# A row softmax on one core: waits put inside the instructions of VectorE and GpSimd, and two 16-row transfers joined into one of 32 rows, in each direction

## The chip, the core and the metric

The kernel runs on one core of a Trainium2 chip. The metric is the device time of one execution in microseconds (us). The kernel before took 159.75 us, the median of three runs (159.71, 159.75 and 159.80). One more execution was profiled, and it took 160.0 us. All engines start together and meet only through semaphores: VectorE (DVE), ScalarE (ACT), GpSimd (POOL) and SyncE (SP), which here only issues transfers. 16 DMA engines move the data.

## What is computed

The input x has 16 x 1024 rows of 512 float32 values. Each row gets its softmax:

```
x_max = np.max(x, axis=-1, keepdims=True)
exp_x = np.exp(x - x_max)
return (exp_x / np.sum(exp_x, axis=-1, keepdims=True)).astype(np.float32)
```

That is 33.55 MB read and 33.55 MB written, and each value is touched once on the way.

## The kernel before, in words

**Tiling.** The 16,384 rows stand as 128 rows in each of 128 partitions. "Row" below means such a row index, 0 to 127, and stands for 128 rows of x. Computation goes by groups of 8 rows: 16 groups, g = 0 to 15, each 128 x 4096 values. Transfers go by blocks of 16 rows (`BLOCKS`): 8 loads and 8 stores of 4096 KB. Within a block one partition's rows lie side by side in DRAM (`in_dram`), so a block of 16 rows is 128 contiguous runs of 32 KB, one run for each partition. One buffer, `held`, keeps 96 rows per partition, 192 KB (`RING = 96`), and everything is done in place in it. Rows 96 to 127 take the places of rows 0 to 31, once those are stored.

**The four steps of a group.** VectorE takes the negative row maximum (`reduce_max`, L168). ScalarE computes exp(x - max) row by row, eight ACTIVATE instructions per group, and adds up the row sums as it goes (the loop at L194 to L199). VectorE takes the reciprocal of the sums (L174). Then GpSimd (groups 0 to 11) or VectorE (groups 12 to 15) multiplies the group by its reciprocals (`tensor_mul`, L176).

**The order of the work** is written out by hand. `ORDER` is the sequence in which SP issues the transfers. The first `AHEAD` entries are loads that wait for nothing; one of them is put ahead of the starting barrier. `AFTER` holds two stores back until a later group is scaled. `VECTOR` is VectorE's sequence, where Mg is the maximum of group g, Pg its reciprocal when GpSimd scales the group, and Vg its reciprocal and the scaling by VectorE itself:

```
AHEAD = 6
AFTER = {(0, 16): 4, (48, 64): 11}
VECTOR = """
    M0 M1 P0 M2 P1 M3 P2 M4 P3 M5 P4 M6 P5 M7 P6 M8 P7 M9 P8 M10 P9 M11
    P10 P11 M12 M13 V12 M14 V13 M15 V14 V15
"""
```

So the store of rows 0 to 15 is issued once group 4 is scaled too, and the store of rows 48 to 63 once group 11 is. SP issues strictly in this order: a store that waits for its groups holds back whatever stands behind it. The load of rows 96 to 111 waits until rows 0 to 15 are stored, and the load of rows 112 to 127 until rows 16 to 31 are.

**Waits.** `take(engine, semaphore, n)` (L114) is an instruction of its own: the engine waits until the semaphore holds at least n, and takes n off it. VectorE has 28 of these: 8 for loads (`loaded`), 16 ahead of the reciprocals (`expd`, which ScalarE raises once per group) and 4 ahead of its own `tensor_mul` (`to_vector`). GpSimd has 12 (`to_pool`), one ahead of each `tensor_mul`. VectorE's own busy instructions are 36: 16 maxima, 16 reciprocals and 4 multiplications.

Of the kernel before, what the change touches and what calls it, by code (L numbers as in the profile page):

```python
# [1 line left out]

# [4 lines left out]

F32 = mybir.dt.float32
EXP = mybir.ActivationFunctionType.Exp
AX = mybir.AxisListType.X  # L10

GROUP = 8
GROUPS = 16
RING = 12 * GROUP

BLOCKS = [(0, 16), (16, 32), (32, 48), (48, 64), (64, 80), (80, 96), (96, 112), (112, 128)]
ORDER = [
    ("L", (0, 16)),
    ("L", (16, 32)),
    ("L", (32, 48)),
    ("L", (48, 64)),
    ("L", (64, 80)),
    ("L", (80, 96)),
    ("S", (0, 16)),
    ("S", (16, 32)),  # L30
    ("S", (32, 48)),
    ("L", (96, 112)),
    ("L", (112, 128)),
    ("S", (48, 64)),
    ("S", (64, 80)),
    ("S", (80, 96)),
    ("S", (96, 112)),
    ("S", (112, 128)),
]
AHEAD = 6  # L40

# [9 lines that stand above are left out]
AT_HEAD = {mybir.EngineType.SP: 1}  # L53

def loads_at_the_head(nc):

    main, body = nc.main_func.blocks[0], nc.main_func.blocks[1]
    for engine, count in AT_HEAD.items():  # L60
        loads = [
            i
            for i in body.instructions
            if i.engine == engine and type(i).__name__ == "InstDMACopy"
        ][:count]
        barrier = next(
            n
            for n, i in enumerate(main.instructions)
            if i.engine == engine and type(i).__name__ == "InstDrain"
        )  # L70
        for load in loads:
            body.instructions.remove(load)
        main.instructions[barrier:barrier] = loads


@with_exitstack
def kernel(
    ctx: ExitStack,
    tc: tile.TileContext,
    x: bass.AP,  # L80
    out: bass.AP,
):
    nc = tc.nc
    nc.at_finalize(loads_at_the_head)
    P = nc.NUM_PARTITIONS

    d = x.shape[-1]
    x_rows, out_rows = x.flatten_outer_dims(), out.flatten_outer_dims()
    assert x_rows.shape[0] == GROUPS * GROUP * P

    def in_dram(rows, a, b):

        first, last = next(k for k in BLOCKS if k[0] <= a and b <= k[1])
        block = rows[first * P : last * P].rearrange("(p r) d -> p r d", p=P)
        return block[:, a - first : b - first, :]

    held = nc.alloc_sbuf_tensor("held", [P, RING, d], F32).ap()
    shift = nc.alloc_sbuf_tensor("shift", [P, GROUPS * GROUP], F32).ap()
    sums = nc.alloc_sbuf_tensor("sums", [P, GROUPS * GROUP], F32).ap()
    recip = nc.alloc_sbuf_tensor("recip", [P, GROUPS * GROUP], F32).ap()  # L100

    loads = [k for what, k in ORDER if what == "L"]
    stores = [k for what, k in ORDER if what == "S"]
    loaded = {k: nc.alloc_semaphore(f"loaded{k[0]}") for k in loads}
    scaled = [nc.alloc_semaphore(f"scaled{g}") for g in range(GROUPS)]
    stored = {k: nc.alloc_semaphore(f"stored{k[0]}") for k in stores}
    maxed = nc.alloc_semaphore("maxed")
    expd = nc.alloc_semaphore("expd")
    to_pool = nc.alloc_semaphore("to_pool")
    to_vector = nc.alloc_semaphore("to_vector")  # L110

    def take(engine, semaphore, n):

        engine.wait_ge(semaphore, n).then_inc(semaphore, -n)  # L114

    def rows(a, b):
        assert a // RING == (b - 1) // RING
        return held[:, a % RING : (b - 1) % RING + 1, :]

    def meets(k, a, b):  # L120
        return k[0] < b and a < k[1]

    def group(g):
        return g * GROUP, (g + 1) * GROUP

    def stats(t, g):
        return t[:, g * GROUP : (g + 1) * GROUP]

    def load(k):
        copy = nc.sync.dma_start(out=rows(*k), in_=in_dram(x_rows, *k))  # L130
        copy.then_inc(loaded[k], 16)
        return copy

    with tc.manual_schedule():
        for _, k in ORDER[:AHEAD]:
            tc.no_tile_sem_insts.add(load(k).ins.name)
    tc.close()  # L140
    tc.compile()  # L141

    taken, done = set(), set()
    for what, k in ORDER[AHEAD:]:
        if what == "L":
            for s in stores:
                if meets(s, k[0] - RING, k[1] - RING) and s not in taken:
                    take(nc.sync, stored[s], 16)
                    taken.add(s)
            load(k)  # L150
        else:
            for g in range(GROUPS):
                if (meets(k, *group(g)) or AFTER.get(k) == g) and g not in done:
                    take(nc.sync, scaled[g], 1)
                    done.add(g)
            nc.sync.dma_start(out=in_dram(out_rows, *k), in_=rows(*k)).then_inc(
                stored[k], 16
            )


    seen = set()

    def rowmax(g):
        for k in loads:
            if meets(k, *group(g)) and k not in seen:
                take(nc.vector, loaded[k], 16)
                seen.add(k)
        nc.vector.reduce_max(  # L168
            out=stats(shift, g), in_=rows(*group(g)), axis=AX, negate=True
        ).then_inc(maxed, 1)  # L170

    def scale(g, engine, ready):
        take(nc.vector, expd, 1)
        nc.vector.reciprocal(out=stats(recip, g), in_=stats(sums, g)).then_inc(ready, 1)  # L174
        take(engine, ready, 1)
        engine.tensor_mul(  # L176
            out=rows(*group(g)),
            in0=rows(*group(g)),
            in1=stats(recip, g).unsqueeze(2).to_broadcast([P, GROUP, d]),
        ).then_inc(scaled[g], 1)  # L180

    for step in VECTOR.split():
        what, g = step[0], int(step[1:])
        if what == "M":
            rowmax(g)
        elif what == "V":
            scale(g, nc.vector, to_vector)
        else:
            scale(g, nc.gpsimd, to_pool)


    nc.scalar.preload_act_table(EXP)  # L192

    with nc.scalar.Fori(0, GROUPS) as i:  # L194
        take(nc.scalar, maxed, 1)
        for r in range(GROUP):
            row = held[:, bass.ds(i % (RING // GROUP) * GROUP + r, 1), :]
            at = bass.ds(i * GROUP + r, 1)
            act = nc.scalar.activation(  # L199
                out=row,  # L200
                in_=row,
                func=EXP,
                bias=shift[:, at],
                scale=1.0,
                accum_out=sums[:, at],
            )
        act.then_inc(expd, 1)


    for k in stores:  # L210
        if k not in taken:
            take(nc.sync, stored[k], 16)


# [1 line left out]
_INS = ['x']  # L216
_OUTS = [((16, 1024, 512), 'float32')]


# [23 lines left out]
```

## Time and profile before

| What | Value |
|---|---|
| profiled execution, its own time | 160.0 us |
| its span, from the first instruction to the last | 158.7 us |
| median of three runs | 159.75 us |
| VectorE busy | 90.1 us (57%), 36 instructions |
| ScalarE busy | 92.0 us (58%), 257 instructions |
| GpSimd busy | 83.9 us (53%), 16 instructions |
| DMA | 2305 packets, 67.12 MB, mean 423 GB/s |

The span ends with SP's wait for the last store; 1.3 us of the profiled execution's time lie outside it. An engine's busy time leaves out its waits and the instructions that only issue transfers. The DMA lines count packets over all 16 engines: each 4096 KB transfer shows as 128 packets of 32768 bytes, 8 on each DMA engine, and 16 packets of 4 bytes, one on each DMA engine, that raise the semaphore of the transfer. The trace records start, duration and size of every packet, and the time at which each transfer has landed (its 16th raise of the semaphore).

For finding one's way by time: the loads land at 12.41, 22.10, 31.81, 41.52, 51.24 and 60.95 us (rows 0 to 95), 99.98 (rows 96 to 111) and 109.69 (rows 112 to 127). The stores land at 70.65, 80.31 and 90.27 us (rows 0 to 47), then at 119.38, 129.22, 139.33, 149.00 and 158.65 us (rows 48 to 127).

### The profile page before, as it was taken

What the parts mean: (1) busy time and instruction counts of PE and PEld (TensorE: products, weight loads), DVE (VectorE), ACT (ScalarE), POOL (GpSimd) and SP (SyncE); (2) the same over time, 40 slices, a digit from 0 to 9 for tenths busy, and PEclk for the clock granted to TensorE, in tenths of its full rate; (3) what the DMA queues carried; (4) which work ended last, traced back from release to release, by engine and by line L of the source; (5) the groups of instructions that cost most, each with busy time, mean ns of one, the idle gap of its engine ahead of it and who ended that gap; (6) DMA issues with size and microseconds to landing.
All of it is one profiled execution on the core that took longest, in us unless ns stands there. A gap on an engine that the chain in (4) does not pass through costs nothing. (4 is left out here: it accounts for less than half of the span.)

```text
span 158.7 us, 747 instructions
## 1 busy us (share of the span) xinstructions
DVE 90.1 (57%) x36; ACT 92.0 (58%) x257; POOL 83.9 (53%) x16
## 2 busy tenths in 40 slices
DVE  0008959778877977977700000794999996820000
ACT  0300699999999999999994000059936749000000
POOL 0000009999999999999999999990000000000000
DMA  8999999999999999999999999999999999999996
GB/s 264 446 463 413 405 463 446 405 430 479 413 396 454 454 413 396 479 446 396 430 479 413 396 396 396 479 446 396 405 520 396 396 446 473 396 405 512 405 405 264
DMA packets 2305, 67.12 MB, mean 423 GB/s; under 512 B 256, under 2 KB 256, under 8 KB 256
## 3 DMA queue, kind: packets, MB, share of 16 engines
q1 hardware_dynamic: 2304, 67.11, 98.9%
q14 instruction: 1, 0.01, 0.0%
HBM read 33.55 MB, written 33.55 MB: 423 GB/s over the span
## 5 line engine op out<-in xcount | busy, mean ns | idle before, releaser
L199 ACT ACTIVATE held<-held,shift x128 | 90.3, 709 | 39.1 <-ACTq L114 39.1
L176 POOL TENSOR_TENSOR held<-held,recip 128x4096 f32<-128x4096 f32 x12 | 83.7, 7018 | 23.2 <-POOLq L114 23.2
L168 DVE TENSOR_REDUCE shift<-held 128x8 f32<-128x4096 f32 x16 | 70.3, 4401 | 27.2 <-DVEq L114 27.2
L199 ACT ACTIVATION_READ_ACCUMULATOR held<-held,shift x128 | 24.2, 189 | 0.0
L176 DVE TENSOR_TENSOR held<-held,recip 128x4096 f32<-128x4096 f32 x4 | 17.7, 4424 | 0.6
L174 DVE RECIPROCAL recip<-sums 128x8 f32<-128x8 f32 x16 | 3.2, 202 | 22.0 <-DVEq L114 22.0
L192 ACT ACT_TABLE_LOAD x1 | 1.3, 1283 | 3.9 <-PEq L141 3.9
L227 POOL MEMSET const-float32-0.0<- 128x1 f32 x1 | 0.1, 99 | 0.2 <-issue 0.2
L227 POOL MEMSET const-bfloat16-1.0<- 128x1 bf16 x1 | 0.1, 103 | 0.0
L227 POOL MEMSET const-uint8-127<- 128x1 uint8 x1 | 0.1, 102 | 0.0
L227 POOL MEMSET const-float32-1.0<- 128x1 f32 x1 | 0.1, 99 | 0.0
## 6 DMA issues: line engine op xcount, KB each, us to landing
held<-in_x_dram SPq DMA_DIRECT2D x8, 4096.0 KB, 30.0
out_dram<-held SPq DMA_DIRECT2D x8, 4096.0 KB, 21.1
```

What stands on the lines that cost most here:

```text
L168: nc.vector.reduce_max(out=stats(shift, g), in_=rows(*group(g)), axis=AX, negate=True).then_inc(maxed, 1)
L174: nc.vector.reciprocal(out=stats(recip, g), in_=stats(sums, g)).then_inc(ready, 1)
L176: engine.tensor_mul(out=rows(*group(g)), in0=rows(*group(g)), in1=stats(recip, g).unsqueeze(2).to_broadcast([P, GROUP, d]),).then_inc(scal ...
L192: nc.scalar.preload_act_table(EXP)
L199: act = nc.scalar.activation(out=row, in_=row, func=EXP, bias=shift[:, at], scale=1.0, accum_out=sums[:, at],)
L227: nc = _bacc.Bacc("TRN2", target_bir_lowering=False, num_devices=1)
```

## The change

Two things are edited. First, the transfers: rows 64 to 95 are one block instead of two, so one load of 8192 KB stands where two of 4096 KB stood, and one store likewise; one run in DRAM for this block is 64 KB long. `AHEAD` is 5, since the same six blocks' worth of rows is now five loads.

Second, the waits: a reciprocal waits for `expd` itself (`wait_op` on the instruction), and a `tensor_mul` waits itself for `to_pool` or `to_vector`. The semaphores are no longer lowered after each wait but count up, so the g-th wait asks for a higher value, and one `take` for each of the three semaphores at the end lowers them to zero. The waits for loads remain instructions of their own, 7 now. VectorE's waits of their own fall from 28 to 9, GpSimd's from 12 to 1.

```diff
-BLOCKS = [(0, 16), (16, 32), (32, 48), (48, 64), (64, 80), (80, 96), (96, 112), (112, 128)]
+BLOCKS = [(0, 16), (16, 32), (32, 48), (48, 64), (64, 96), (96, 112), (112, 128)]
...
-    ("L", (64, 80)),
-    ("L", (80, 96)),
+    ("L", (64, 96)),
...
-    ("S", (64, 80)),
-    ("S", (80, 96)),
+    ("S", (64, 96)),
...
-AHEAD = 6
+AHEAD = 5
...
-    seen = set()
+    seen, given = set(), {}
...
     def scale(g, engine, ready):
-        take(nc.vector, expd, 1)
-        nc.vector.reciprocal(out=stats(recip, g), in_=stats(sums, g)).then_inc(ready, 1)
-        take(engine, ready, 1)
+        nc.vector.reciprocal(out=stats(recip, g), in_=stats(sums, g)).wait_op(
+            expd, g + 1, "sem-ge"
+        ).then_inc(ready, 1)
+        given[ready] = given.get(ready, 0) + 1
         engine.tensor_mul(
             out=rows(*group(g)),
             in0=rows(*group(g)),
             in1=stats(recip, g).unsqueeze(2).to_broadcast([P, GROUP, d]),
-        ).then_inc(scaled[g], 1)
+        ).wait_op(ready, given[ready], "sem-ge").then_inc(scaled[g], 1)
...
+    take(nc.vector, expd, GROUPS)
+    take(nc.vector, to_vector, given[to_vector])
+    take(nc.gpsimd, to_pool, given[to_pool])
```

Order and number of the busy instructions are the same on every engine; SP issues 14 transfers instead of 16.

## Prediction, made before the changed kernel ran

> **What bounds the kernel now.** I first read the page's span and its DMA queues:
>
> ```profile
> span 158.7 us, 747 instructions
> q1 hardware_dynamic: 2304, 67.11, 98.9%
> q14 instruction: 1, 0.01, 0.0%
> ```
>
> The data queue keeps 16 DMA engines busy for 98.9% of the span, while no compute engine passes 58%. The second line is the bound; the third, a single packet of instructions, matters below. Next the busy time by stretch, to see whether the DMA engines ever run dry:
>
> ```profile
> core 0: us, DVE busy (x) ACT busy (x) POOL busy (x), PEclk, DMA share, GB/s
> ...
> 20.00:60.00 40.00, 31.37 (x15) 40.00 (x115) 36.33 (x6) 1.00 1.00 433
> 60.00:85.00 25.00, 15.38 (x8) 25.00 (x72) 25.00 (x4) 1.00 1.01 434
> 85.00:95.00 10.00, 0.20 (x1) 0.13 (x2) 10.00 (x3) 1.00 1.03 419
> ...
> 140.00:157.00 17.00, 0.00 (x0) 0.00 (x0) 0.00 (x0) 1.00 1.00 432
> ```
>
> The last columns: a DMA share of 1.00 and 432 to 434 GB/s, with VectorE busy or not. Only 85 to 95 us is slower (419): packets there last up to 2.17 us, on all 16 engines at once. So a compute engine counts only where it issues a transfer too late. There are two tight places. The store of rows 0 to 15 is issued at 58.69 (group 4 scaled); the first DMA engine to finish the loads goes on with it at 59.80 and the last at 60.51. The store of rows 48 to 63 is issued at 107.50 (group 11); its first packets start at 108.99. From issue to first packet the first load took 1.02 us, so the slack is 0.09 to 0.80 us in the first place and 0.47 us or more in the second.
>
> The chain of waits ends on VectorE at 139.9 and says nothing here: the last store is issued at 140.0 and queues behind others until 158.65.
>
> **How the DMA engines end.** In the packet records an engine starts a 32 KB packet every 1.21 us (1.213 long, overlapping the next by 4 ns), a semaphore packet of 9 ns costs its engine 5 ns, and 14 engines end between 157.40 and 157.68 us. Two are late: one ends at 157.91, one at 158.23, and the kernel ends with that one (landing at 158.65). Its history shows why. At 130.94 it took the instruction packet:
>
> ```profile
> q1 hardware_dynamic: 15, 0.49, 94.8%
> q14 instruction: 1, 0.01, 1.6%
> ```
>
> (DMA view, 130.0 to 131.2 us.) This 8192-byte packet took 0.309 us, the next data packet began 0.306 us late and took 1.564 us instead of 1.213: 0.66 us in all. Stepping back from its end at 158.23 by 1.21 us a packet leads exactly to that packet. Without it this engine would have ended at 157.57, and the last would be the one at 157.91, which collects small delays (14 to 69 ns a packet) during stores.
>
> **Who fetches instructions at 130.94?** By the instruction records GpSimd had run its last instruction by then (started 100.39), SP had waited since 125, and ScalarE was in the 16th turn of a loop whose first 15 turns fetched nothing. VectorE had started its 66th of 70 at 129.14:
>
> ```profile
> 128.80 0.19 DVE L174 RECIPROCAL recip<-sums 128x8 f32<-128x8 f32 x1
> 129.14 4.42 DVE L176 TENSOR_TENSOR held<-held,recip 128x4096 f32<-128x4096 f32 x1
> 135.13 0.20 DVE L174 RECIPROCAL recip<-sums 128x8 f32<-128x8 f32 x1 [1.56 <-DVEq L114]
> ```
>
> It also has the longest program without a loop. So I take the fetch as VectorE's, set off by the count of instructions that it has passed. That is inferred, not shown.
>
> **The change part by part.**
>
> *Waits inside instructions.* VectorE loses 16 + 4 waits and one load's wait, and gains two at the end: 70 records become 51. It never comes to a 66th, so no fetch falls in the span (SP goes from 47 to 44, GpSimd from 40 to 29). The end moves from 158.23 to 157.91: **-0.32 us**. Bounds: 0, if the fetch is another engine's; -0.66, if the engine at 157.91 catches up too.
>
> A wait instruction of its own costs about 0.11 us ahead of a reciprocal (23.11 to 23.22). GpSimd's come early, under the instruction before: its multiplications start 6.975 us apart and last
>
> ```profile
> L176 POOL TENSOR_TENSOR held<-held,recip x12: 7017/7018/7019, 23.7 to 100.4; 128x4096 f32<-128x4096 f32 x12
> ```
>
> so they already run without a gap. At most the chain starts 0.1 to 0.2 us earlier, and the two tight stores with it. They queue behind loads anyway: 0. Behind a waiting GpSimd instruction stand only its later multiplications; behind VectorE's waiting reciprocal stand the maxima that stood behind the wait before.
>
> *The load.* The same bytes in the same queue land together at about 60.95, so rows 64 to 79 come 9.7 us later. Group 8's maximum, at 57.22 before, starts at 61.1 and ends at 65.5; group 7's reciprocal behind it moves from 62.71 to 65.5. GpSimd needs it at 72.50: 7.0 us spare. ScalarE starts group 8 about 3 us late and stays so through group 11, whose reciprocal moves from 85.27 to about 88.5; GpSimd wants it at 100.39. Group 12 waits for its load (99.98) in any case. Cost 0; it would show only if the load came over 6 us later still.
>
> *The store.* Rows 64 to 95 are scaled by 107.4, and both old stores were issued by 108.5, behind the store of rows 48 to 63. Cost 0. The freed SP time (0.34 us per issue, 1.00 for the third) hid under transfers: 0.
>
> *Packets.* If a 64 KB run is one packet, each DMA engine has 16 fewer data packets and 2 fewer semaphore packets. The trace has no 64 KB packet. The nearest row for a packet's fixed cost is the semaphore packet: 9 ns long, 5 ns of its engine's time. 18 x 5 ns = **-0.09 us**; ends of the range for this part 0 and -0.16 (18 x 9 ns). The other way, long packets might run slower: the slowest stretch (419 against 433 GB/s, 3.2%) over 32 of 128 packets, 38.8 us, would be +1.25.
>
> *Sum*: -0.32 - 0.09 = -0.41 us. The profiled execution's 160.0 becomes 159.6, its span 158.3. The profiled execution stands 0.25 above the median of the runs; 159.75 - 0.41 = 159.34, so I forecast 159.35 us.
>
> **The rivals.**
>
> *The fetch costs nothing, or stays.* For it: that VectorE fetches is inferred, and 1.8 us pass between its last instruction and the packet. Only -0.09 is left: 159.65. Against: the delayed DMA engine is the last one. The Trainium skill, "Runtime: NRT & Kernel Launch", section "Instruction fetch mechanics", speaks against this change's gain: crossing into the next block of instructions costs one tail-bump and is "mostly hidden". By that rule the sum would be -0.09. It gives 16 KiB blocks; this trace's packet has 8192 bytes, and VectorE indeed did not stall.
>
> *Slower: 64 KB runs cost bandwidth.* Place: the one load and the one store. Price: 3.2% of 38.8 us, +1.25, so 160.6; from a loss of 1.1% on them it eats up the 0.41. Against: the 32 KB runs show no loss, at 433 GB/s. The Trainium skill, "DMA: Bandwidth & Descriptors", section "Latency and other measured facts", has copies at a row pitch of 512 KiB at 207 GB/s against 214 with padding, and much slower from 2 MiB on. The pitch here goes from 32 to 64 KB, below all that this page of the Trainium skill lists; no trace so far shows what it does.
>
> *Slower: GpSimd wakes late from each embedded wait.* From the end of the first reciprocal to the first multiplication pass 0.26 us. Paid 12 times, it is 3.1 us at the store of rows 48 to 63, less 0.5 of slack: +2.6, 162.0. It decides from about 0.06 us per multiplication. Against: from the second on, the reciprocal is ready 1.5 us or more before the multiplication ahead has ended (29.10 against 30.65, then 5.64 against 6.975 per group), so nothing has to wake.
>
> *Much faster: a transfer has a fixed cost.* 1.02 us from issue to first packet, twice: 157.3. Against: queued loads land 9.70 apart, and 8 x 1.21 us are 9.68. The Trainium skill, "DMA: Bandwidth & Descriptors", section "Anatomy of one DMA", fits a fixed cost of about 2.0 us per transfer, for transfers issued from GpSimd; two fewer would by that be about 4 us less, an estimate that the landings here speak against.
>
> *It doesn't do what it says:* the long run is cut into 32 KB packets. Then only the fetch goes: 159.4.
>
> **How the numbers follow.** Forecast (with the cut run, and the late engine's share) 0.54, own range 159.1 to 159.5; fetch without worth 0.32; bandwidth 0.09; late GpSimd 0.03; fixed cost 0.02. Within 0.2% means within 0.32 us, about what a measurement of this kernel can tell from no change. Of the forecast's 0.54, I put 0.09 within that bound, since -0.41 is close to it. So faster 0.47, same 0.32 + 0.09 = 0.41, slower 0.12. The range 159.0 to 159.9 holds the first two cases with their bounds and leaves out the rest, some 0.15 to 0.2.
>
> **What would show it.** No q14 line in the span, and 2016 DMA packets (14 x 144; 2272 if the run is cut), with the last two DMA engines 0.3 us apart or less. Group 8's maximum near 61.1, group 7's reciprocal near 65.5, GpSimd's multiplications still about 6.975 apart, the two tight stores issued by 58.7 and 107.5. A q14 line that remains proves the first step wrong; packets of 64 KB longer than 2.43 us the second; a GB/s below 430 in 52 to 61 or 120 to 139 us speaks for lost bandwidth.

## The result, and the profile after

The changed kernel took **160.41 us**, the median of 22 runs (159.56 to 161.35); the kernel before took 159.82 us beside it (22 runs, 159.70 to 161.05). The ratio is 1.0029, with a 95% interval of 1.0016 to 1.0043. I had forecast 159.35 us and a range of 159.0 to 159.9: it became slower, not faster. Two things are already in these numbers. The fastest execution of the changed kernel is 0.14 us faster than the fastest of the kernel before. And its executions lie far apart: 20 of 22 runs of the kernel before stay below 160.1 us, while 16 of 22 of the changed kernel lie above 160.15.

The profiled execution is one of the long ones, 161.07 us. Its page:

```profile
span 159.8 us, 714 instructions
DMA packets 2016, 67.11 MB, mean 420 GB/s; under 512 B 224, under 2 KB 224, under 8 KB 224
q1 hardware_dynamic: 2016, 67.11, 97.9%
```

There are 2016 packets, as forecast for 64 KB packets, and no q14 line: the instruction packet is gone. But the data queue is busy for 97.9% of the span instead of 98.9%. VectorE, around the load of rows 64 to 95 (start, duration, and in brackets the idle time before):

```profile
56.73 0.21 DVE L172 RECIPROCAL recip<-sums 128x8 f32<-128x8 f32 x1 [1.15 <-ACT held L202]
60.75 4.42 DVE L167 TENSOR_REDUCE shift<-held 128x8 f32<-128x4096 f32 x1 [3.82 <-DVEq L112]
65.09 0.19 DVE L172 RECIPROCAL recip<-sums 128x8 f32<-128x8 f32 x1
```

Group 8's maximum waits 3.82 us for the joined load and starts at 60.75; group 7's reciprocal comes at 65.09. Both are as forecast (61.1 and 65.5), and GpSimd never noticed:

```profile
L176 POOL TENSOR_TENSOR held<-held,recip x12: 7015/7016/7017, 23.1 to 99.9; 128x4096 f32<-128x4096 f32 x12
```

Twelve multiplications, first start 23.1 and last 99.9: still 6.975 us apart. They began 0.53 us earlier than before, however. Of that, 0.24 us is an earlier first load in this execution (12.17 instead of 12.41), the rest goes with the two embedded waits: from the landing of the first load to the first multiplication pass 10.97 us here and 10.98 in e1 (waits alone, below), 11.26 before and 11.27 in e2 (transfers alone). SP's issues follow (start, time over all of them, line, how many):

```profile
0.00 2.63 SPq L128 DMA_DIRECT2D held<-in_x_dram  x5
58.16 7.30 SPq L154 DMA_DIRECT2D out_dram<-held  x3
70.43 10.16 SPq L128 DMA_DIRECT2D held<-in_x_dram  x2
106.96 34.00 SPq L154 DMA_DIRECT2D out_dram<-held  x4
```

The first store is issued at 58.16 instead of 58.69. In the kernel before the same line was:

```profile
58.69 7.30 SPq L156 DMA_DIRECT2D out_dram<-held  x3
```

I had seen that coming, though smaller, and had costed it at nothing.

**Where the time is.** The DMA view of 157.4 to 159.8 us in the changed kernel; one digit is 0.06 us:

```profile
DMA  0000000000009000000000000000000000000000
DMA packets 5, 0.03 MB, mean 14 GB/s; under 512 B 4, under 2 KB 4, under 8 KB 4
```

15 of the 16 DMA engines start no data packet any more (4 of them still raise their semaphore). One engine starts another 32 KB packet at 158.17. The end of the kernel waits for that one. In the kernel before, nothing but semaphore packets starts in the same stretch:

```profile
DMA packets 15, 0.00 MB, mean 0 GB/s; under 512 B 15, under 2 KB 15, under 8 KB 15
```

When the late engine fell behind can be read from the semaphore raises, one for each DMA engine, that the trace keeps for every transfer:

| raised (us), first / middle / last engine | before | changed |
|---|---|---|
| store of rows 0 to 15 | 70.05 / 70.24 / 70.65 | 69.83 / 70.14 / 70.34 |
| store of rows 32 to 47 | 89.82 / 90.10 / 90.27 | 89.67 / 89.89 / 90.04 |
| load of rows 96 to 111 | 99.65 / 99.83 / 99.98 | 99.15 / 99.50 / **101.18** |
| last store | 157.74 / 157.94 / 158.65 | 157.21 / 157.55 / **159.72** |

The middle engine ends 0.39 us *earlier* than before. (That is not the fetch, which held up a single engine. Of the 0.39 us, 0.10 are there at the store of rows 0 to 15, and 0.23 more arise up to the load of rows 96 to 111, by a smaller loss at that switch.) The last engine falls behind between 90 and 101 us, where the queue goes over from three stores to the load of rows 96 to 111: it starts its first packet of that load at 90.68, about 1.0 us after finishing the store, and the packet takes 1.70 us instead of 1.213. So my theory for the experiments: *everything that was forecast happened, and something makes single DMA engines fall behind at this switch*. The rivals: the long packets do it; the embedded waits or the missing fetch do it; or it is the time at which the first store is issued, which the embedded waits moved.

### The profile page after: what moved, and what is told of

Same layout as the page of the kernel before. It is cut to its first block, busy times and chain, and to the rows that moved or that the text cites. A ratio compares the mean times of both kernels' runs of the same rounds, so it can differ in the third digit from the quotient of the medians.

```text
span 159.8 us, 714 instructions
## 1 busy us (share of the span) xinstructions
DVE 90.0 (56%) x36; ACT 92.1 (58%) x257; POOL 83.9 (53%) x16
## 2 busy tenths in 40 slices
DMA packets 2016, 67.11 MB, mean 420 GB/s; under 512 B 224, under 2 KB 224, under 8 KB 224
## 3 DMA queue, kind: packets, MB, share of 16 engines
q1 hardware_dynamic: 2016, 67.11, 97.9%
## 5 line engine op out<-in xcount | busy, mean ns | idle before, releaser
L202 ACT ACTIVATION_READ_ACCUMULATOR held<-held,shift x128 | 24.7, 193 | 0.0
## 6 DMA issues: line engine op xcount, KB each, us to landing
held<-in_x_dram SPq DMA_DIRECT2D x1, 58.4
```

The costliest lines, as they stand in the source:

```text
L202: act = nc.scalar.activation(out=row, in_=row, func=EXP, bias=shift[:, at], scale=1.0, accum_out=sums[:, at],)
```

## The experiments

Each kernel was timed in five rounds against the kernel before. The last column of the tables counts executions above 160.15 us; of the runs of the kernel before beside them, 3 to 7 of 29 to 35 lie there, and none of 16 beside the last two kernels. The medians of the kernel before beside them are 159.88 to 159.93 us. The ratio and its interval are estimated from all runs, so the ratio is not quite the quotient of the medians.

**First: the parts.** The edits, against the changed kernel (e1, e3, e4) and the kernel before (e2):

```diff
e1: BLOCKS, ORDER, AHEAD of the kernel before; waits of the changed kernel
e2: BLOCKS, ORDER, AHEAD of the changed kernel; waits of the kernel before
e3: one load of rows 64 to 95, two stores
-    ("S", (64, 96)),
+    ("S", (64, 80)),
+    ("S", (80, 96)),
e4: two loads, one store of rows 64 to 95
-    ("L", (64, 96)),
+    ("L", (64, 80)),
+    ("L", (80, 96)),
-AHEAD = 5
+AHEAD = 6
```

> The waits inside the instructions, with the transfers of before (16 transfers, 32 KB runs). Theory L (the long transfers make one DMA engine fall behind by 1 to 2 us in most executions): no such engine here and no instruction packet in the span, so about 159.5 us, 0.2% below before, with executions no further apart than those of before (some 0.4 us). Theory W (the waits or the missing instruction fetch do it): about 160.4 us like the changed kernel, executions 1 to 2 us apart, one DMA engine ending over 1 us after the others.

> One transfer of 32 rows each way, with the waits of before as instructions of their own. Theory L: executions 1 to 2 us apart, median 160.4 to 160.9 us, one DMA engine over 1 us late at the end of the profile; the instruction packet (one on q14) is still there, late in the span. Theory W: about 159.7 us, tight, the packet there too.

> The changed kernel with rows 64 to 95 still loaded by one transfer of 64 KB runs, but stored by two of 32 KB runs (64 KB apart in DRAM). If the long load alone causes the late engine: 160.3 to 160.5 us and as scattered as the changed kernel. If the long store alone: 159.5 us and tight. Theory W: 160.4 us.

> The changed kernel with rows 64 to 95 loaded by two transfers of 32 KB runs (64 KB apart in DRAM), and stored by one of 64 KB runs. If the long store causes the late engine: 160.3 to 160.5 us and scattered. If the long load alone: 159.5 us and tight. In the changed kernel's profile the engine fell behind at 90.7 us, before the long store was issued (107.6), which speaks for the load. Theory W: 160.4 us.

| | median us (range, runs) | ratio to before, interval | above 160.15 |
|---|---|---|---|
| e1 waits alone | 160.02 (159.37 to 160.74, 12) | 1.0006 (0.9989 to 1.0022) | 6 |
| e2 transfers alone | 159.98 (159.84 to 161.67, 12) | 1.0017 (0.9996 to 1.0037) | 5 |
| e3 long load, two stores | 160.20 (159.67 to 160.93, 12) | 1.0020 (1.0003 to 1.0036) | 6 |
| e4 two loads, long store | 160.01 (159.41 to 160.94, 12) | 0.9997 (0.9974 to 1.0020) | 4 |

Neither theory held. The scatter comes with the waits alone and, weaker, with the transfers alone; e1's expectation by the long transfers (tight) and e2's by the waits (tight) both failed. Two readings survive. The profile of e1, at 159.37 us its fastest execution, has no instruction packet, and that is 0.30 us below the fastest run of before (159.67). And in all profiles so far the time follows the last engine: 0.5 to 0.6 us after the middle one and 159.4 us (e1), 1.3 us and 160.1 (e4), 1.4 us and 160.5 (e2), 2.1 to 2.2 us and 160.9 to 161.1 (e3, changed). In e2 and e3 the late engine, too, stands idle before its first packet of the load of rows 96 to 111 (it starts at 90.14 and 90.32), and that packet takes 1.77 and 1.94 us. What went along with the scatter was the issue of the first store: 58.16 (e1), 58.10 (e3), 58.35 (e4), 58.59 (e2), 58.69 (before).

**Second: the time of the first store, and where the lag begins.**

```diff
e5 (against the changed kernel); spare has 384 values per partition
+    nc.gpsimd.memset(spare, 0.0).wait_op(to_pool, 1, "sem-ge")
e6 (against the kernel before)
-AFTER = {(0, 16): 4, (48, 64): 11}
+AFTER = {(0, 16): 3, (48, 64): 11}
e7 (against the changed kernel)
-    ("S", (32, 48)),
     ("L", (96, 112)),
     ("L", (112, 128)),
+    ("S", (32, 48)),
e8 (against e1): ahead of VECTOR's first step
+    for i in range(19):
+        nc.vector.memset(spare[:, i : i + 1], 0.0)
```

> The changed kernel with a memset of 384 values per partition on GpSimd ahead of its first multiplication, so that the whole chain of multiplications, and with it the two held-back stores, runs some 0.5 us later, as in the kernel before (58.7 instead of 58.16 us). Theory P (phase: the earlier store makes one DMA engine fall behind at the switch from stores to loads near 88 us): 159.5 us and executions within 0.5 us. Theory D (the lag is a draw that this issue time does not steer): 160.2 to 160.5 us and scattered over 1 us or more, as the changed kernel.

> The kernel before, with the store of rows 0 to 15 held back only until group 3 is scaled: issued near 51.7 us instead of 58.7. Theory P: scattered, 160.3 us or more. Theory D: as the kernel before, 159.8 us and mostly within 0.4 us.

> The changed kernel with the store of rows 32 to 47 put behind the loads of rows 96 to 111 and 112 to 127 in SP's order, so that the stores give way to loads at about 80 us instead of 90. If the stretch of slow packets on all 16 DMA engines near 88 us belongs to this switch, it moves to about 78 us, and the lag of single engines begins there; if it belongs to the time since the start or to the store of rows 32 to 47, it stays near 88 us or moves with that store to about 106. Median between 159.6 and 160.5 us, since there is still one such switch.

> The waits inside the instructions with the transfers of before, and 19 memsets of one value per partition at the head of VectorE's program, in its idle time before the first load lands: VectorE's 66th record comes again, near 129 us. If that count sets off the instruction fetch: one packet on q14 near 130 to 131 us, its DMA engine about 0.65 us late afterwards, the fastest execution at about 159.7 us instead of 159.37. If the fetch is another engine's: none, and 159.4 us for the fastest. If embedded waits as such scatter the executions: over 1 us apart in any case; if the missing fetch does: as tight as the kernel before.

| | median us (range, runs) | ratio to before, interval | above 160.15 |
|---|---|---|---|
| e5 changed, GpSimd later | 159.82 (159.69 to 160.27, 12) | 0.9997 (0.9986 to 1.0007) | 2 |
| e6 before, store at 51.65 | 160.18 (160.00 to 160.58, 12) | 1.0018 (1.0009 to 1.0027) | 8 |
| e7 changed, loads sooner | 161.37 (160.96 to 161.71, 6) | 1.0088 (1.0071 to 1.0106) | 6 |
| e8 waits alone, 19 memsets | 160.02 (159.48 to 160.78, 12) | 1.0007 (0.9989 to 1.0026) | 5 |

e5 answers the main question in the direction of phase: a delay of half a microsecond takes the scatter away. The median is not the 159.5 that I had expected of it, though. e6 was a miss in its form: an issue 7 us early does cost 0.3 us, but evenly, within 0.6 us, and not by a late engine. Its busy time by stretch, beside the kernel before (last column GB/s; e6 first):

```profile
86.00:92.00 6.00, 0.00 (x0) 0.00 (x0) 6.00 (x2) 1.00 1.01 437
```

```profile
86.00:92.00 6.00, 0.00 (x0) 0.00 (x0) 6.00 (x2) 1.00 0.91 350
```

With a store waiting in the queue well ahead, the packets just ahead of the first switch are slow (all 16 that start from 58.6 to 59.2 take 1.39 to 2.15 us, where before none is over 1.25), and the second switch, which moves 350 GB/s in the kernel before, runs at 437. e7 says that the slow stretch belongs to the switch: with the loads put ahead of the third store it moved from 88 to 78 us, a second one came at 96 to 99 where the stores begin again, and the whole was slower (161.37, outside the 159.6 to 160.5 that I had expected). In e8 the instruction packet is back:

```profile
q1 hardware_dynamic: 16, 0.52, 82.8%
q14 instruction: 1, 0.01, 1.3%
```

(DMA view, 115.5 to 117 us.) Only VectorE's program was made longer, so the fetch is VectorE's. It came at 116.06, 14 us sooner than expected, and the fastest execution, 159.48, did not show the 0.3 us that I expected of it: it is 0.11 above the fastest of e1. The scatter stayed, so the missing fetch is not its cause.

**Third: the first store alone.** SP also waits for a semaphore that VectorE raises; GpSimd, the other stores and all waits stay.

```diff
f1 (against the changed kernel); spare has 1536 values
+            if k == (0, 16):
+                take(nc.sync, hold, 2)
...
+    nc.vector.memset(spare, 1.0).then_inc(hold, 1)
...
+        if step == "M8":
+            nc.vector.reduce_max(out=top, in_=spare, axis=AX).wait_op(
+                hold, 1, "sem-ge"
+            ).then_inc(hold, 1)
f2 (against e1): the memset on GpSimd of e5
f3 (against the kernel before); SP takes 1 off hold where f1 takes 2
-AFTER = {(0, 16): 4, (48, 64): 11}
+AFTER = {(48, 64): 11}
...
+        if step == "M8":
+            nc.vector.memset(spare, 0.0).then_inc(hold, 1)
f4: the changed kernel
```

> The changed kernel with the store of rows 0 to 15 alone held back: SP also waits for a 1536-value maximum of a spare tile on VectorE, put in VectorE's idle time ahead of the maximum of group 8 (about 57.0 to 58.7 us). GpSimd's chain and the other stores keep the early times of the changed kernel (65.1 and 107.0 us); the first store is issued near 58.75 us instead of 58.16. Theory S (it is the issue of this store, about 0.5 us too early, that makes single DMA engines fall behind at the switch near 88 us): 159.8 us, three in four executions within 0.4 us. Theory G (it is the phase of GpSimd's chain or of the later stores): 160.2 to 160.5 us, scattered over 1 us or more.

> The waits inside the instructions with the transfers of before, and the memset on GpSimd that delays its chain by some 0.5 us. By either phase theory this is tight like the kernel before, without its instruction fetch. If the fetch's 0.3 us still counts: 159.5 to 159.6 us. If the shared delay at the switch near 88 us eats it up, as with the long transfers and the same delay: 159.8 us.

> The kernel before, with the first store released by a one-value memset on VectorE behind the reciprocal of group 6, so that it is issued near 57.4 us instead of 58.7; nothing else moves. Theory S: executions scattered over 1 us or more, median 160.2 us or more. Theory G: as the kernel before, 159.8 to 159.9 us, mostly within 0.4 us.

> The changed kernel itself on this chip, so that the three others have it beside them: 160.2 to 160.6 us, scattered over 1 us or more; the profile's time follows the last DMA engine: span about 157.4 us plus how far the last engine ends after the middle ones, plus some 0.4 to 0.5.

| | first store | median us (range, runs) | ratio to before, interval | above 160.15 |
|---|---|---|---|---|
| f1 changed, store held | 58.74 | **159.79** (159.51 to 160.05, 11) | 0.9991 (0.9982 to 1.0001) | 0 |
| f2 waits alone, GpSimd later | 58.82 | 159.79 (159.60 to 161.35, 12) | 0.9993 (0.9973 to 1.0013) | 1 |
| f3 before, store early | 57.20 | 159.81 (159.52 to 160.03, 11) | 0.9991 (0.9981 to 1.0001) | 0 |
| f4 changed kernel again | 58.12 | **160.44** (159.60 to 161.36, 12) | 1.0029 (1.0010 to 1.0049) | 8 |

f1 against f4, on one chip, is the decisive pair. SP's issues in f1, and what holds the first of them:

```profile
0.00 2.62 SPq L131 DMA_DIRECT2D held<-in_x_dram  x5
58.74 6.83 SPq L159 DMA_DIRECT2D out_dram<-held  x3
70.56 9.99 SPq L131 DMA_DIRECT2D held<-in_x_dram  x2
107.08 32.79 SPq L159 DMA_DIRECT2D out_dram<-held  x4
```

```profile
56.94 1.70 DVE L191 TENSOR_REDUCE top<-spare 128x1 f32<-128x1536 f32 x1
```

The first two stores go out 0.58 us later; the third store and the store of rows 48 to 63 keep the changed kernel's times (65.2 and 107.1), as does GpSimd (first multiplication at 23.26). The median falls by 0.65 us and the scatter is gone. It is not the added instructions that do it: g2, below, has the same ones with a shorter maximum, and is as slow as the changed kernel. At the load of rows 96 to 111 the last engine is now 0.33 us behind the middle one (99.75, 100.08). So the rival with GpSimd's phase, or that of the stores behind the first two, is out. (The second store goes out behind the first in SP's order and moves with it.) f4's profile is an execution of 159.65 us, and shows the rule of the first table once more: middle engine 157.47, last 158.30, against 157.55 and 159.72 in the one of 161.07 us. Of the 1.42 us between these two executions of one kernel, 1.34 are the last engine's lag (2.17 less 0.83) and 0.08 the middle engine.

f3 was a miss: the store at 57.20 did no harm to the kernel before. Early as such is not bad.

**Fourth: the shape, and what the long load has to do with it.** The edits are those of f1 or f3, with other sizes of the spare tile (1216 values in g2, 1984 in g3, 736 in g4 and h1) and on other kernels: g1 is f3's edit on the changed kernel, g4 f1's edit on the kernel before in place of group 4's release, h1 the same on e2, h2 f3's edit on e1.

> The changed kernel with the first store released behind the reciprocal of group 6, so issued near 57.1 us instead of 58.16. If only a window near 58.1 to 58.4 us is bad: tight, and without the instruction fetch some 0.2 to 0.3 us below the kernel before with the same early store (159.81): 159.5 to 159.6 us. If early issue is bad as such and the kernel before is protected by something else: 160.2 us or more, scattered.

> The changed kernel with the first store held until about 58.4 us (a 1216-value maximum on VectorE). Window theory: at its edge, about half of the executions above 160.15 us, median 160.0 us. If the bad times end sharply at the early side of 58.4: 159.8 us and tight.

> The changed kernel with the first store held until about 59.2 us (a 1984-value maximum). The first packets of the store can then start near 60.2 us, and the first DMA engines have finished the loads by 59.7: these wait up to 0.5 us, those that finish last hardly. Tight, 159.8 to 160.0 us.

> The kernel before, all waits and transfers as they were, with the first store alone released earlier, near 58.2 us, by a 736-value maximum on VectorE. Window theory: scattered over 1 us or more, median 160.2 us or more, as the changed kernel: the early issue alone does it. If the waits or the long transfers are needed as well: 159.8 us, tight.

> The joined transfers with the waits of before, and the first store alone released near 58.2 us by a 736-value maximum on VectorE (without it: 58.6 us, 159.98 us). If the long load and the early store together make the loss: 160.3 us or more, scattered over 1 us or more. If the embedded waits are needed too: 159.9 to 160.0 us.

> The waits inside the instructions with the transfers of before, and the first store released behind the reciprocal of group 6, near 57.1 us. If the joined transfers are worth the 0.09 us that their fewer packets save: 159.6 us, 0.1 above the changed kernel with the same early store (159.53). If the long load is harmful here too: 159.3 to 159.4 us.

| | load of rows 64 to 95 | first store (profile) | median us (range, runs) | ratio to before, interval |
|---|---|---|---|---|
| g1 changed | one, 64 KB | 57.14 | **159.53** (159.27 to 160.13, 12) | 0.9979 (0.9969 to 0.9988) |
| g2 changed | one, 64 KB | 58.66 | 160.46 (159.60 to 161.33, 11) | 1.0032 (1.0013 to 1.0051) |
| g3 changed | one, 64 KB | 59.26 | 160.20 (160.02 to 160.32, 11) | 1.0016 (1.0008 to 1.0025) |
| g4 before | two, 32 KB | 58.14 | 159.93 (159.60 to 160.35, 11) | 0.9999 (0.9982 to 1.0016) |
| h1 joined transfers, old waits | one, 64 KB | 58.11 | **160.64** (159.96 to 161.26, 6) | 1.0057 (1.0042 to 1.0072) |
| h2 waits alone | two, 32 KB | 57.25 | **159.53** (159.25 to 159.77, 10) | 0.9977 (0.9967 to 0.9986) |

SP's first three stores in g1, g2, g4, h1 and h2, in this order:

```profile
57.14 8.43 SPq L158 DMA_DIRECT2D out_dram<-held  x3
58.66 7.14 SPq L159 DMA_DIRECT2D out_dram<-held  x3
58.14 7.83 SPq L161 DMA_DIRECT2D out_dram<-held  x3
58.11 7.84 SPq L159 DMA_DIRECT2D out_dram<-held  x3
57.25 8.41 SPq L160 DMA_DIRECT2D out_dram<-held  x3
```

With the long load there is a bad window: 57.14 is the fastest, 58.11 to 58.66 are bad and scattered (f4, h1, g2), 58.74 is good again (f1), and 59.26 is even but late. In g3 the DMA engines that finish the load first wait for the store, so that the 16 raises draw together from 0.50 us apart to 0.26. Its middle engine ends at 158.46, in f1 at 157.78; of these 0.68 us, 0.19 are there at the first store and 0.35 more arise up to the load of rows 96 to 111. g2 and g3 were misses: I had expected 159.8 or 160.0 and 159.8 to 160.0. The late edge of the window is known only roughly, since each time is that of one profiled execution, and the issue moves with the landing of the first load, which lies between 12.10 and 12.51 us in the profiles. In g2's it came latest, 0.23 us after f1's; with f1's landing, g2's store would go out near 58.4.

In g2's profile two engines are over 1.5 us late, and they show the picture of the changed kernel: both start their first packet of the load of rows 96 to 111 at 90.30 and 90.31, some 0.7 us after the store, and it takes 1.70 and 1.68 us. In f1 and g1 every engine goes on at once.

The load decides how much the early issue costs, but two short loads are not free of it. With the waits of before and the store near 58.1, one long load and store give 1.0057 of the kernel before (h1), and two give 0.9999 (g4, whose executions lie somewhat wider; its expectation of 160.2 or more failed). With the embedded waits the store near 58.1 stands against the one near 57.2 as 1.0029 against 0.9979 with one load (f4, g1) and as 1.0006 against 0.9977 with two (e1, h2). Over all kernels with the store between 58.1 and 58.7 us, except the kernel before itself and e7 with its other order, the ratios are 0.9997 to 1.0007 with two loads (e4, g4, e1, e8) and 1.0017 to 1.0057 with one (e2, e3, the changed kernel, f4, g2, h1). The intervals of e2 and e3 overlap those of the first group, so the division is plain only for the other four. That it is the load and not the joined store of the same rows is shown by time: the changed kernel issues that store at 107.56, when its engine is already late. h1 needs no embedded wait for it; its page still has VectorE's fetch:

```profile
q1 hardware_dynamic: 2016, 67.11, 98.7%
q14 instruction: 1, 0.01, 0.0%
```

g1 and h2 beat both kernels of this case, the one before by 0.2% and the changed one by more. They have the embedded waits and the store out of the window. Between them, the joined transfers make no difference (I had expected h2 0.1 above or 0.1 to 0.2 below g1).

## Why the prediction was wrong, point by point

**The bound** was right: the last DMA engine to finish sets the end, in every profile here.

**The fetch** was right in kind; what it is worth is not settled. It is VectorE's (e8), and the embedded waits remove it. In all seven profiles that have it the packet takes 0.309 us and the data packet behind it 0.35 to 0.47 us longer than its like, so the delay of its DMA engine was right. It comes after 62 to 66 of VectorE's records (66 before, 62 in e8), so it is not set off by one fixed count of them, as I had taken it. For its worth the cleanest pair is f3 and h2, which differ in the waits alone and have the first store out of the window: 159.81 and 159.53 us, each on its own chip, or 0.14% by their ratios to the kernel before (0.9991 and 0.9977; their intervals overlap a little), 0.22 us; the fastest runs of before and e1 differ by 0.30. I had said 0.32. Not all of this need be the fetch, since the pair differs in all 32 moved waits. The Trainium skill, "Runtime: NRT & Kernel Launch", section "Instruction fetch mechanics", calls such a fetch mostly hidden. It is hidden from VectorE, but not from its DMA engine, which ended last in the profile of the kernel before. I had sized the term from that one profile. In g4 and f3 another engine ends within 0.15 us of it, and in e2, e6, e8 and h1 another ends 0.25 to 0.72 us later. So the fetch sets the end only where no other engine is later.

**The packets** were right where they matter little. A 64 KB packet takes 2.418 us, twice 1.213 less 8 ns; I had said below 2.43. The -0.09 us that I expected is too small for these runs to show: g1 and h2 have the same median.

**The rival of lost bandwidth** did not happen. The changed kernel by stretch, without the long load and with it (last column GB/s):

```profile
20.00:40.00 20.00, 14.81 (x9) 20.00 (x58) 16.86 (x3) 1.00 1.01 437
40.00:60.00 20.00, 13.53 (x7) 20.00 (x57) 20.00 (x4) 1.00 1.01 437
```

The 64 KB packets, which fill the second line, move as much as the 32 KB ones. The sign that I had named for it, a GB/s below 430, was ill chosen: 52 to 61 us reads 411, but so does the kernel before, and 120 to 139 us reads 429 against 435 before, although the 64 KB packets of the load and of the store take 2.419 and 2.420 us on average. The price was misread too: I had called 85 to 95 us the only slower stretch (419), while rows that I left out read 417 to 446 from 95 to 140 us; what is slow are the packets near 87.7 us. The 32 KB packets at a pitch of 64 KB (e3, e4) took 1.213 to 1.214 us like all others, so what the Trainium skill says of a large row pitch ("DMA: Bandwidth & Descriptors", section "Latency and other measured facts") does not begin at 64 KB here.

**The other rivals** did not happen either: GpSimd did not wake late (6.975 us between multiplications), and two transfers fewer saved no microseconds.

**The step that failed** is the sentence on the tight stores: "At most the chain starts 0.1 to 0.2 us earlier, and the two tight stores with it. They queue behind loads anyway: 0." It put the earlier issue at nothing because the store waits in the queue in any case. The chain started 0.53 us earlier in the profiled executions, 0.29 of it from the waits, and the price was not 0 but 0.65 us in the median (f4 less f1), more than the 0.41 us that I had hoped to gain. I had measured the slack of this store to the late side (0.09 us for the first DMA engine) and never asked for the early side. I had taken it that a transfer that queues behind others cannot cost anything; here its issue time changes how evenly the 16 engines get through a change of direction 30 us later. The joined load failed with it. Its late landing cost nothing, as forecast, but "Cost 0" for the load as a whole was wrong: with it the early issue costs more (h1 against g4, f4 against g1 beside e1 against h2).

**Of the signs that I had named**, these came as forecast: packets, no q14, group 8's maximum, group 7's reciprocal, the 6.975 us and the issue of the two tight stores. The GB/s is spoken of above. The one that failed was that the last two DMA engines end 0.3 us apart or less: they ended 1.4 us apart.

**What stays open.** Shown is that the issue time of the first store decides (f1, f4), that the long load is needed for the full loss (g4, h1), and that most of the lag arises at the switch from stores to the load near 88 to 101 us. Why is not shown. One thing fits the edges of the window, and is only argued: the store's first packet can start 1.02 us after its issue, as the first load did. Issued at 57.14 us (g1), it is there at 58.16, when the DMA engines are in the first half of their last 64 KB packet of the load, and six of these packets do take 2.72 to 3.01 us there, where none is over 2.44 in f1, g2 and h1; issued at 58.74 (f1), at 59.76, when the first of them has just finished that packet (59.70); issued at 58.11 to 58.66 (h1, g2), at 59.13 to 59.68, in its second half, before any has finished. With 32 KB packets the last one is half as long. These times, too, are good to a few tenths at best, by what was said of the first landing. How that should come back 30 us later, I can't say.

## What to carry to other kernels

In a kernel bound by its transfers, ask of each DMA engine when it ends, not of the queue when it is full: in the changed kernel one engine that falls behind sets the time, while the middle engine ends earlier than before. A gain of some tenths of a microsecond anywhere on the chain that releases a transfer moves that transfer, and neither earlier nor later need be better: here 51.65 us (e6) and 59.26 (g3) cost time, and so does a window between good places. After such a change, place the release again (g1: with this one store issued 1 us sooner the changed kernel goes from 1.0029 to 0.9979 of the kernel before). Look at the spread of the executions beside their median: here it showed the new mechanism before any profile did.

## What the runs showed of the hardware

- Where the queue goes over from stores to loads near 90 us, 7 to 16 of the 16 DMA engines slow down together in the last packet ahead of the switch: packets of 1.3 to 2.4 us instead of 1.213, starting from 87.5 to 88.4 us, in all profiles but two. In e7, where the switch was moved, they start near 78 us, and in e6 there are none.
- At the switch from loads to stores near 60 us such packets show only where the first store was issued at 57.2 us or earlier: 1.39 to 2.15 us in e6, 1.33 to 1.62 in f3, and 64 KB packets of 2.72 to 3.01 in g1 (in h2, at 57.25, a single one of 1.36).
- An engine that is over 1.5 us late at the end stood idle between the store and its first packet of the next load, and that packet was slow (the changed kernel, e3, g2). How evenly the switch hits the engines differs between executions of one kernel: the last ended 2.17 us after the middle one in one of the changed kernel, 0.83 in another (f4).
- Removing 20 waits from VectorE's program removed its instruction fetch from the span; 19 memsets at its head brought it back.
